# Column chunks of both array halves side by side in the expert weights of block 1

## The chip, the cores and the metric

The kernel runs on one core of a Trainium2 chip. The metric is the time of one execution on the device in microseconds (us); less is better. Before the change, three runs gave a median of 2655.25 us (2653.65 to 2655.34).

## The reference, cut to what matters

Two transformer blocks follow one another on 256 tokens of 1024 channels, in float32. The change touches the feed-forward part of block 1: 16 experts, each of which takes its best 34 tokens and applies a gated product with a hidden width of 2816.

```python
def _expert_choice_ffn(h, norm_g, w_router, w_gate, w_up, w_down):
    ...
    hid = (jax.nn.silu(jnp.einsum('becd,edf->becf', xs, w_gate))
    ...
```

So for every expert `silu(xs @ w_gate) * (xs @ w_up)` is formed, [tokens, 2816], and multiplied with `w_down` [2816, 1024]. Each hidden column goes through this on its own, and the sum over hidden columns may be taken in any order. Block 2 has a context stream (256 context tokens, whose only product is a few states of two recurrences) and a latent stream, which needs block 1's output.

## The kernel before, in words

The kernel has three parts. `head` is block 1's token mixer and router. `ffn` (L787) is block 1's experts, and in the same stage the context stream of block 2 (`ctx_pre`, from L885), which depends on no expert. `lat` is the rest of block 2 and waits for the last expert's result.

An expert (`expert`, L836) has room for 64 tokens, so a product fills only half of TensorE's columns. Two products therefore run on the two halves of the array. The 2816 hidden columns are cut in two halves of 1408; the lower half of the array takes the first, the upper half the second. A loop over three chunks takes 512, 512 and 384 columns of each half. For each chunk, `w_gate` and then `w_up` are multiplied with the tokens: eight k-tiles of 128 channels, at each the product of half 0 and then that of half 1 (`gu`, L848). Then come the sigmoid on ACT and two products on DVE (`hid`), transposes (`hb`, L858), a copy (`hT`), and the second product into `dn` (L866). The next expert's tokens are gathered (`xg`, `xt`, `ohb`) in the second chunk, and `sc` (L879, L880) adds the result to the tokens. A float32 matmul of the program stands in the trace as two.

Weights come through ten slots of 8 KB a partition (1 MB each), which are used in turn; the first expert has four more. `wload` (L223) loads [1024, n] weights. For n of 512 or 384 it puts four k-tiles of one half into one slot:

```python
        kk = SLOTW // n if n <= 256 else 4
        kk = min(kk, KD)
```

So a chunk of `w_gate` comes in four loads: half 0 with k-tiles 0 to 3, half 0 with 4 to 7, then the same of half 1. A row of such a load is 2048 B (512 columns) or 1536 B (384). `rload` (L244) loads rows of `w_down`, 4096 B each, two k-tiles a slot; the 384 rows of a half's third chunk take one full and one half-filled slot. Loads are issued on SP's queue, in the program's order, and a load waits there until the last matmul that read its slot is done.

The order of the instructions on each engine is fixed when the program is built: a scheduler puts them in order by its own estimate of when each could start, and so spreads the context stream's work between the experts' matmuls. On the chip every engine runs its list in order. The context stream's work on PE is, in this order: projections (`pc`), an inverse by steps (`gic`, `gib`, `giy`; later `r0ic`, `r0ib`, `r0iy`), and scans (`gp`; `rp`). Each step's matmul waits for DVE or ACT to have processed the step before. A step of the inverse on PE (L1104) is one of three: with `gY` (or `rY`) as the first operand, then with `giZ` (`r0iZ`), then with `ctab`.

Of the kernel before, what the change touches and what calls it, by code (L numbers as in the profile page):

```python
# [50 lines left out]
# blocks of 2048 modulation columns and channel tiles, in the order in which they are taken  # L51
# [4 lines left out]
# weight slots that the first expert has besides  # L56
RX = 4
# products queued behind those of the solves and scans: of the next column tile, and others
# [26 lines left out]
def const_table():  # L85
# [3 lines left out]
    # pairs of neighbouring blocks of 2^l  # L89
# [54 lines left out]
class Ring(list):  # L144
    """pools of weight slots, used in turn"""
# [7 lines left out]
class Net:  # L153
    def __init__(self, tc, I, out, ctx, ring=4):
# [7 lines left out]
        # what the mixers alone need, apart  # L162
# [19 lines left out]
    def add_ring(self, ctx, name, n):  # L182
        """n weight slots of 8 KB a partition, handed out in turn with those that are there"""
        pool = ctx.enter_context(self.tc.tile_pool(name=name, bufs=n, reuse_waits="tile"))
        self.rings = Ring(self.rings + [pool] * n)

    @contextmanager
    def phase(self, **banks):
        """PSUM banks by tag, for a part of the kernel"""
        old = self.rings, self.ptag  # L190
        with ExitStack() as ctx:
            self.pspool = {t: ctx.enter_context(self.tc.tile_pool(name=t, bufs=n, space=PSUM, reuse_waits="tile")) for t, n in banks.items()}
            yield ctx
        self.rings, self.ptag = old

    @contextmanager
    def side(self, pool, tag):
        """emit with weight slots of `pool` and the PSUM banks of `tag`"""
# [24 lines left out]
    def wload(self, src, n):  # L223
        """[1024, n] weights as a function of the k-tile and the columns"""
        kk = SLOTW // n if n <= 256 else 4
        kk = min(kk, KD)
# [7 lines left out]
    def loader(self, bufs):  # L234
        """128 columns of block 2's input projection (or n of src) at a time, into bufs of 4 KB a partition in turn"""
# [9 lines left out]
    def rload(self, src):  # L245
        """rows of 1024 columns, 128 a k-tile"""
# [9 lines left out]
    def split(self, src, hi, lo, eng=None):  # L256
        """an exact split of float32 values in two parts of fewer bits"""
        self.nc.scalar.copy(hi, src)  # L258
        (eng or self.nc.vector).tensor_sub(lo, src, hi)  # L259
        return hi, lo  # L260

    def product3(self, out, pairs):
        """out = the sum of a^T b over pairs of operands in two parts each; the product of the second parts is below
        the last bit"""
# [5 lines left out]
    def sigmoid(self, out, x, scale=1.0, nbias=None):  # L270
        """1 / (1 + exp(-(scale x + bias))); nbias holds -bias"""
# [5 lines left out]
    def rsqrt_cols(self, out, x, scale, bias):  # L277
        """out = (x*scale + bias) ** -0.5 through exp and ln."""
# [4 lines left out]
    def evac(self, out, src, scale=None, eng=None):  # L283
        """PSUM to SBUF, alternating between ACT and DVE."""
# [12 lines left out]
    def head(self):  # L297
        tc, nc, I = self.tc, self.nc, self.I
        ring = self.rings[0]
        # the weights' slots of both parts of the block  # L300
# [13 lines left out]
    def norm_rows(self, W, src, tag):  # L314
        """x * rsqrt(mean(x^2) + eps) for the token tiles in src."""
# [16 lines left out]
    def to_T2(self, W, src, gain, name):  # L332
        """token tiles -> [128, 8, 272] in two parts, channel on partitions, scaled per channel; the meta tokens also whole"""
# [13 lines left out]
    def wgroup(self, src, c):  # L347
        """256 columns of [1024, n] weights, whole and in two parts"""
# [9 lines left out]
    def metas(self, W, um, raw):  # L358
        """[16, 256]: the meta tokens' products with whole weights, the channels in four parts at once"""
# [10 lines left out]
    def head_body(self, W):  # L370
# [31 lines left out]
        # log_sigmoid of the decay logits, on every partition  # L402
# [4 lines left out]
        def rvt(t, name):  # L407
            """in place of states to come, where there are any"""
# [10 lines left out]
        # projections, channel-major  # L419
# [25 lines left out]
        # decayed scores of the retention  # L445
# [10 lines left out]
        # token-major projections  # L456
# [6 lines left out]
        def projN(c0, out):  # L463
            """256 columns of all tokens at a time"""
# [21 lines left out]
        # retention  # L486
# [34 lines left out]
        # what bars a direction from the tokens on its other side, in place of the distances  # L521
# [3 lines left out]
        # the gates' columns in two parts, spread so that the two directions start at partitions 0 and 32  # L525
# [6 lines left out]
        # gates  # L532
# [35 lines left out]
        # matrix memory: weighted scores of both directions, and the sums over them a head later  # L568
# [62 lines left out]
        # output projection and residual; the retention's gate on the way  # L631
# [28 lines left out]
        # the router's logits on the way: products with the channels as they come, the norm's factor later  # L660
# [31 lines left out]
    def head_norm(self, W, out, src, n, name):  # L692
        """(x - mean) * rsqrt(var + eps) over each of four heads of 128."""
# [11 lines left out]
    def log_sigmoid(self, W, out, x, n, m, name):  # L705
        """min(x, 0) - log1p(exp(-|x|))"""
# [11 lines left out]
    def route(self, W, h, lT):  # L718
        """softmax over experts, the best CAP tokens of each, one-hot maps."""
# [58 lines left out]
    def norm_factor(self, W, x, junk, t, n):  # L778
        """rsqrt(mean(x^2) + eps) of the rows of a token tile"""
# [9 lines left out]
    def ffn(self):  # L789
        with self.front, self.phase(pa=6, pb=2) as ctx:  # L790
# [4 lines left out]
            # more slots at first, in place of the context's tiles to come  # L795
# [9 lines left out]
    def gather(self, W, e):  # L805
        """the tokens of an expert, channel-major, and the way back"""
        nc = self.nc
        # one-hot rows of the places, twice: for both halves of the channels
# [27 lines left out]
    def expert(self, W, e, tokens):  # L836
# [4 lines left out]
        for c, (f0, w) in enumerate(((0, 512), (512, 512), (1024, 384))):  # L841
            gu = []
            for src in (I["w_gate"], I["w_up"]):
                b = self.bank("gu")
                ws = [self.wload(src[0, e, :, h * (DFF // 2) + f0:h * (DFF // 2) + f0 + w], w) for h in range(2)]
                for k in range(KD):
                    for h in range(2):
                        nc.tensor.matmul(b[h * 64:(h + 1) * 64, :w], xs[:, k, :], ws[h](k),  # L848
# [11 lines left out]
            self.evac(hT[:, :nf], hb[:, :nf], eng="v" if c % 2 else "s")  # L860
            for h in range(2):
                r0 = h * (DFF // 2) + f0
                wd = self.rload(I["w_down"][0, e, r0:r0 + w, :])
                for j in range(nf):
                    for dc in range(2):
                        nc.tensor.matmul(dn[dc * 64:(dc + 1) * 64], hT[:, j, h * 64:(h + 1) * 64],  # L866
                                         wd(j, slice(dc * 512, (dc + 1) * 512)),
# [18 lines left out]
    def ctx_pre(self):  # L886
        """modulation vectors and the states that the context stream leaves behind"""
# [7 lines left out]
        with tc.tile_pool(name="CW", bufs=2, reuse_waits="tile") as CW, self.side(CW, "pb"):  # L895
            with tc.tile_pool(name="C", bufs=1, reuse_waits="tile") as C:
                with tc.tile_pool(name="C0", bufs=1, reuse_waits="tile") as T:
                    # what the shift adds to the logits of the routing to come
# [27 lines left out]
    def ada(self, W):  # L926
        """modulation vectors of both streams: channel columns, and the rows that gate the residuals; a step per weight slot"""
# [19 lines left out]
        def close(c):  # L947
            """rows of 512 columns at every 32nd partition, for the context one partition on"""
# [41 lines left out]
    def gate_rows(self, which, out):  # L990
        """broadcast one residual gate over the partitions: [128, 1024]"""
# [10 lines left out]
    def mod_cols(self, W, gain, r, shift, scale, name):  # L1002
        """gain * (1 + scale) and shift as channel columns."""
# [7 lines left out]
    def norm256(self, W, src, dst, name):  # L1011
        """dst = src * rsqrt(mean(src^2) + eps) for two token tiles [128, 1024]"""
# [11 lines left out]
    def affT(self, W, src, gs, sh, name, tag=None, ptags=None):  # L1024
        """two token tiles -> [128, 8, 256] with channels on partitions, times gs plus sh"""
# [15 lines left out]
    def projc(self, w, uT):  # L1041
        """[128 channels, 256 tokens] of one column tile; a step per product"""
# [6 lines left out]
    def advance(self, queue, n):  # L1049
        """emit n steps of what waits in a queue"""  # L1050
# [9 lines left out]
    def fill(self, ins, *steps):  # L1060
        """products that wait for nothing, behind an instruction whose result takes its time"""
# [4 lines left out]
    def softplus(self, W, x, n, m, name):  # L1066
        """x <- max(x, 0) + log1p(exp(-|x|))"""
# [11 lines left out]
    def mixed_inverse(self, W, N, U, d, Y, levels, pfx, hop=lambda ins: None):  # L1079
        """Y = (I + N)^-1 of four strictly triangular 128-blocks [128, 4, 128], in blocks of up to 2^levels. A step per  # L1080
        product.
# [1116 lines left out]
```

## Time and profile before, and how to read it

| what | value |
|---|---|
| median of three runs | 2655.25 us |
| the profiled execution: span from first to last instruction | 2657.6 us |
| the experts' stage (first `gu` to last `sc`), from the span's start | 320.7 to 1854 us |
| PE busy, of the span | 2371.7 us (89%) |
| DVE, ACT, POOL busy | 1145.6, 651.1, 473.6 us |
| loaded by SP's queue | 747.67 MB |
| `gu` matmuls (L848) | 3072, 731.4 us |
| `dn` matmuls (L866) | 1408, 321.1 us |

The profile is one execution, and it gives the span alone as that execution's time. PE is TensorE's matmuls, PEld its weight loads. An engine's busy time is the time in which at least one of its instructions runs. "DMA share" is the mean busy share of the core's 16 DMA engines; as transfers overlap on an engine, it can be over 1. The granted clock is given as a share of full speed (1.00 is 2.4 GHz, and the lower level is 1.2 GHz).

### The profile page before, as it was taken

The page shows a single profiled execution, that of the slowest core. Times are in us where ns is not written, and L with a number is a line of the kernel's source. Part 1 is how long each engine was busy: PE and PEld are TensorE (multiplying, and loading weights), DVE is VectorE, ACT ScalarE, POOL GpSimd, SP SyncE. Part 2 cuts the span into 40 slices and gives each one's busy share as a digit, 9 for nine tenths or more (in the row PEclk, how much of TensorE's full clock was granted, in tenths as well). Part 3 has the DMA queues.
Part 4 walks back from the last instruction along what each step waited for, and adds up shares of the span by engine and source line. Part 5 has one row for each costly group of instructions (what it writes and reads, how often), then busy time and mean ns, then how long its engine had stood idle before and what let it go on. Part 6 is the DMA issues. An engine that isn't in the chain of part 4 may idle for free. (4 is left out here: it accounts for less than half of the span.)

```text
span 2657.6 us, 37500 instructions
## 1 busy us (share of the span) xinstructions
PE 2371.7 (89%) x14784; PEld 1268.7 (48%) x14784; DVE 1145.6 (43%) x2515; ACT 651.1 (24%) x1652; POOL 473.6 (18%) x657
## 2 busy tenths in 40 slices
PE   6879799999999998989989988887898988989997
PEld 5746434334334334334333332222766676876554
DVE  7786311332332333233323321011677866565555
ACT  3334111210211212112112211001453443522222
POOL 5671100100001111011101100000434442210000
PEclk9878899999999999999999999999899999999999
DMA  6537899998989999999989999999221111589995
GB/s 205 188 129 240 287 387 387 385 369 309 382 320 359 354 339 359 358 329 374 359 319 356 368 332 390 394 391 356 70 74 42 28 49 41 169 285 349 365 365 196
DMA packets 426708, 754.58 MB, mean 284 GB/s; under 512 B 13344, under 2 KB 233168, under 8 KB 423456
## 3 DMA queue, kind: packets, MB, share of 16 engines
q1 hardware_dynamic: 425024, 747.67, 79.2%
q0 software_dynamic: 1504, 4.46, 0.5%
q8 instruction: 119, 1.95, 0.3%
q14 instruction: 61, 0.50, 0.1%
HBM read 751.03 MB, written 1.05 MB: 283 GB/s over the span
## 5 line engine op out<-in xcount | busy, mean ns | idle before, releaser
L848 PE MATMUL gu<-w,xs 128*64 128x512 f32 (+1 forms) x3072 | 731.4, 584 | 33.5 <-DMA w<-in_w_up 19.9
L848 PEld LDWEIGHTS gu<-w,xs 128*64 128x64 f32 x3072 | 232.6, 142 | 418.9 <-issue 362.1
L866 PE MATMUL dn<-w,hT 128*64 128x512 f32 x1408 | 321.1, 597 | 11.6 <-ACT hT L290 10.4
L866 PEld LDWEIGHTS dn<-w,hT 128*64 128x64 f32 x1408 | 95.3, 136 | 183.5 <-issue 160.3
L1045 PE MATMUL pc<-luT,w 128*128 128x256 f32 x688 | 176.5, 399 | 1.4 <-DMA w<-in_w_in 1.1
L1045 PEld LDWEIGHTS pc<-luT,w 128*128 128x128 f32 x688 | 127.6, 195 | 23.9 <-issue 4.5
L273 ACT ACTIVATE hid<-gu 128x512 f32<-128x512 f32 (+1 forms) x48 | 26.9, 561 | 403.2 <-PE gu L848 403.2
L2054 PE MATMUL egu<-w,exs 128*64 128x256 f32 x1024 | 123.2, 383 | 0.0
L853 DVE TENSOR_TENSOR hid<-hid,gu 128x512 f32<-128x512 f32 (+1 forms) x48 | 30.7, 639 | 208.9 <-ACT hid L275 208.8
L854 DVE TENSOR_TENSOR hid<-hid,gu 128x512 f32<-128x512 f32 (+1 forms) x48 | 30.8, 643 | 195.3 <-PE gu L848 195.2
L1589 POOL TENSOR_SCALAR rsw<-rSU,rwc 64x64 f32<-64x64 f32 x112 | 40.5, 362 | 332.5 <-DVE rSU L1603 323.5
L2054 PEld LDWEIGHTS egu<-w,exs 128*64 128x64 f32 x1024 | 74.6, 136 | 39.4 <-issue 6.9
L268 PE MATMUL pj<-uTh,wp 128*128 128x272 f32 x320 | 68.3, 308 | 12.1 <-DVE rtmp L441 7.5
L1045 PE MATMUL pc<-cuT,w 128*128 128x256 f32 x288 | 70.3, 392 | 0.0
L2081 PE MATMUL edn<-w,ehT 128*64 128x512 f32 x256 | 67.7, 597 | 0.7 <-ACT ehT L290 0.5
L258 ACT CAST wp<-w 128x1024 fp32r<-128x1024 f32 (+1 forms) x48 | 55.4, 1186 | 49.3 <-DMA w<-in_w_in 33.8
L1098 DVE TENSOR_TENSOR r0iZ<-r0ic,stab 128x512 f32<-128x512 f32 x48 | 32.9, 686 | 78.7 <-PE r0ic L1104 78.6
L259 DVE TENSOR_TENSOR wp<-w,wp 128x1024 fp32r<-128x1024 f32 (+1 forms) x44 | 62.6, 1447 | 9.8 <-ACT wp L258 9.8
L1547 PE MATMUL rmt<-rT,rBK 128*128 128x128 f32 (+1 forms) x256 | 49.8, 341 | 18.7 <-DVE rBK L1515 5.6
L981 POOL TENSOR_TENSOR adac<-adac,w 128x2048 f32<-128x2048 f32 x14 | 66.1, 4722 | 0.3
L1045 PEld LDWEIGHTS pc<-cuT,w 128*128 128x128 f32 x288 | 53.5, 193 | 19.1 <-issue 10.6
L268 PEld LDWEIGHTS pj<-uTh,wp 128*128 128x128 f32 x320 | 55.2, 205 | 14.4 <-issue 8.1
(686 smaller groups left out, 3740.5 us busy)
## 6 DMA issues: line engine op xcount, KB each, us to landing
w<-in_w_down SPq DMA_DIRECT2D x160, 1024.0 KB, 11.4
w<-in_w_gate SPq DMA_DIRECT2D x128, 1024.0 KB, 10.3
w<-in_w_up SPq DMA_DIRECT2D x128, 1024.0 KB, 11.6
w<-in_w_gate SPq DMA_DIRECT2D x64, 768.0 KB, 8.3
w<-in_w_up SPq DMA_DIRECT2D x64, 768.0 KB, 7.1
w<-in_w_in SPq DMA_DIRECT2D x65, 512.0 KB, 4.1
w<-in_moe_w_gate SPq DMA_DIRECT2D x32, 1024.0 KB, 13.4
w<-in_moe_w_up SPq DMA_DIRECT2D x32, 1024.0 KB, 12.1
```

The lines of the kernel that those rows point to most:

```text
L258: self.nc.scalar.copy(hi, src)
L259: (eng or self.nc.vector).tensor_sub(lo, src, hi)
L268: self.nc.tensor.matmul(out, a[x], b[y], start=(i == 0 and x + y == 0), stop=(i == n - 1 and x == 1))
L848: nc.tensor.matmul(b[h * 64:(h + 1) * 64, :w], xs[:, k, :], ws[h](k), start=(k == 0), stop=(k == KD - 1))
L866: nc.tensor.matmul(dn[dc * 64:(dc + 1) * 64], hT[:, j, h * 64:(h + 1) * 64], wd(j, slice(dc * 512, (dc + 1) * 512)), start=(c == 0 and h = ...
L981: nc.gpsimd.tensor_add(acc[c], acc[c], w)
L1045: self.nc.tensor.matmul(b, w(k), uT[:, k, :], start=(k == 0), stop=(k == KD - 1))
L1098: nc.vector.tensor_tensor(out.rearrange("p u (i c) -> p u i c", i=4), x.unsqueeze(2).to_broadcast([P, 4, 4, 32]), blk, op=ALU.mult)
L1547: ins = nc.tensor.matmul(b[:, i], BK[:, c0 + i, h:h + 2, :], T[:, h, c0 + i, :, :], start=True, stop=True)
L1589: nc.gpsimd.tensor_scalar(sw[r], SU[r, h, c, :], wc[r, c:c + 1], 0.0, op0=ALU.mult, op1=ALU.add)
L2054: nc.tensor.matmul(b[64 * i:64 * i + 64, x * 256:x * 256 + 256], xs[:, k, i, :], w[i](k), start=(k == 0), stop=(k == KD - 1))
L2081: nc.tensor.matmul(b[64 * i:64 * i + 64, :], hT[:, j, 64 * i:64 * i + 64], wd[i](j, cs), start=(j == 0), stop=(j == 1))
```

## The change

The two halves of the array take neighbouring columns. The chunks are now of 1024, 1024 and 768 neighbouring hidden columns; in each chunk half 0 takes the first 512 (or 384) columns and half 1 the next. `wload` is called once for both halves, and loads two k-tiles of 1024 (768) columns into a slot, in rows of 4096 (3072) B. The rows of `w_down` are taken in the same new order, 1024, 1024 and 768 at a time. Every product is still formed, over other groups of columns.

```diff
     def wload(self, src, n):
-        kk = SLOTW // n if n <= 256 else 4
-        kk = min(kk, KD)
+        kk = min(SLOTW // n, KD)
...
-        for c, (f0, w) in enumerate(((0, 512), (512, 512), (1024, 384))):
+        for c, (f0, w) in enumerate(((0, 512), (1024, 512), (2048, 384))):
...
-                ws = [self.wload(src[0, e, :, h * (DFF // 2) + f0:h * (DFF // 2) + f0 + w], w) for h in range(2)]
+                ws = self.wload(src[0, e, :, f0:f0 + 2 * w], 2 * w)
                 for k in range(KD):
                     for h in range(2):
-                        nc.tensor.matmul(b[h * 64:(h + 1) * 64, :w], xs[:, k, :], ws[h](k),
+                        nc.tensor.matmul(b[h * 64:(h + 1) * 64, :w], xs[:, k, :], ws(k, slice(h * w, (h + 1) * w)),
...
+            wd = self.rload(I["w_down"][0, e, f0:f0 + 2 * w, :])
             for h in range(2):
-                r0 = h * (DFF // 2) + f0
-                wd = self.rload(I["w_down"][0, e, r0:r0 + w, :])
                 for j in range(nf):
...
-                                         wd(j, slice(dc * 512, (dc + 1) * 512)),
+                                         wd(h * nf + j, slice(dc * 512, (dc + 1) * 512)),
```

The other users of `wload` have 256 columns, for which the number of k-tiles in a slot stays eight.

The scheduler orders the changed program differently. Three places show it.

The first is PE in the third expert, in the context stream's first inverse (`gic`). Before:

```order
L866 MATMUL dn<-w,hT 64x512 x16
L1104 MATMUL gic<-ctab,giB 32x128 x4
L848 MATMUL gu<-w,xs 64x512
L1104 MATMUL gic<-gY,giB 32x128 x4
L1104 MATMUL gic<-giZ,giB 32x128 x4
L1104 MATMUL gic<-ctab,giB 32x128 x4
L1104 MATMUL gic<-gY,giB 32x128 x4
L1104 MATMUL gic<-giZ,giB 32x128 x4
L1104 MATMUL gic<-ctab,giB 32x128 x4
L1104 MATMUL gic<-gY,giB 32x128 x4
L848 MATMUL gu<-w,xs 64x512 x8
```

The same in the changed program:

```order
L1103 MATMUL gic<-gY,giB 32x128 x4
L848 MATMUL gu<-w,xs 64x512 x4
L1103 MATMUL gic<-giZ,giB 32x128 x4
L1103 MATMUL gic<-ctab,giB 32x128 x4
L848 MATMUL gu<-w,xs 64x512 x4
L1103 MATMUL gic<-gY,giB 32x128 x4
L848 MATMUL gu<-w,xs 64x512 x4
L1103 MATMUL gic<-giZ,giB 32x128 x4
L1103 MATMUL gic<-ctab,giB 32x128 x4
L848 MATMUL gu<-w,xs 64x512 x4
```

Before, a `gu` group begins with one matmul alone (that of half 0 at the first k-tile), and the rest follows in pieces of seven, eight or more. Now the pieces are of four, the matmuls that read one slot. Counted from the first expert's `gu` to the context stream's last matmul on PE:

| on PE, in the program's order | before | changed |
|---|---|---|
| pieces of `gu` between other work | 184 | 208 |
| of these, pieces of a single matmul | 50 | 1 |
| L1104 step with `giZ`/`r0iZ` with no expert's matmul ahead of it since the step it depends on (of 48) | 14 | 1 |
| the step with `gY`/`rY`, likewise (of 48) | 16 | 12 |
| the step with `ctab`, likewise (of 36) | 11 | 15 |
| `hb` straight behind `gu` | 4 | 7 |
| `dn` straight behind `hb` | 7 | 11 |

The second place is PE at the end of the context stream's work, the last scan steps (`rp`). Before, this stands in the 13th expert's third chunk:

```order
L1599 MATMUL rp_10638<-rSU_10470,rKt_10477 64x64 x2
L1579 MATMUL rp_10647<-rSU_10470,rT_8614 64x64 x2
L1593 MATMUL rp_10655<-rP_10650,rY_10494 64x64 x2
L848 MATMUL gu<-w,xs 64x384 x8
L1599 MATMUL rp_10655<-rSU_10470,rKt_10477 64x64 x2
L848 MATMUL gu<-w,xs 64x384 x7
L858 MATMUL hb<-ctab,hid 128x128 x3
L866 MATMUL dn<-w,hT 64x512 x12
L879 MATMUL sc<-yhi,ohT 128x512 x4
```

In the changed program it stands in the 12th expert's first chunk:

```order
L848 MATMUL gu<-w,xs 64x512 x4
L1578 MATMUL rp_10615<-rSU_10438,rT_8582 64x64 x2
L1592 MATMUL rp_10623<-rP_10618,rY_10462 64x64 x2
L858 MATMUL hb<-ctab,hid 128x128 x4
L1598 MATMUL rp_10623<-rSU_10438,rKt_10445 64x64 x2
L865 MATMUL dn<-w,hT 64x512 x16
L848 MATMUL gu<-w,xs 64x512 x32
L858 MATMUL hb<-ctab,hid 128x128 x4
```

From there to the end of the stage PE has experts' work alone: before for the rest of one chunk and three experts, now for two chunks and a `dn` and four experts.

The third place is SP's queue at the end of the stage. Before, the third chunk of the last expert's `w_down` comes in four loads, two of them half-filled, and two loads of block 2's `w_in` stand ahead of the last:

```order
L252 DMA w<-in_w_down 128x2x1024
L252 DMA w<-in_w_down 128x1024
L252 DMA w<-in_w_down 128x2x1024
L241 DMA w<-in_w_in 128x8x128 x2
L252 DMA w<-in_w_down 128x1024
L241 DMA w<-in_w_in 128x8x128 x4
```

In the changed program these are three full loads, and `w_in` comes behind them:

```order
L251 DMA w<-in_w_down 128x2x1024 x4
L229 DMA w<-in_w_gate 128x2x768 x4
L229 DMA w<-in_w_up 128x2x768 x4
L251 DMA w<-in_w_down 128x2x1024 x3
L240 DMA w<-in_w_in 128x8x128 x6
```

Behind the stage the order of the work is as it was, but for a few rows.

## Rows read from the trace of the kernel before

**Rows 1.** The page's head.

```profile
span 2657.6 us, 37500 instructions
```

**Rows 2.** Windows of the experts' stage: us, busy us of each engine, PEclk, DMA share, GB/s.

```profile
318.00:583.00 265.00, 251.59 (x1283) 104.53 (x1284) 66.84 (x151) 47.78 (x109) 12.27 (x14) 0.97 1.04 379
583.00:1583.50 1000.50, 915.13 (x5359) 383.39 (x5361) 320.56 (x707) 179.47 (x447) 122.04 (x253) 0.97 0.96 348
1583.50:1854.00 270.50, 221.89 (x986) 73.92 (x982) 28.04 (x47) 23.84 (x40) 0.58 (x1) 0.96 1.04 387
```

**Rows 3.** Waits of PE, 318 to 1583.5 us: total us, times, longest us.

```profile
PE r0ic L1104 <- DVE r0iZ L1098: 8.2, 10, 0.9
...
PE hb L858 <- DVE hid L854: 7.2, 16, 0.8
...
PE dn L866 <- ACT hT L290: 6.0, 12, 1.0
...
PE gic L1104 <- DVE giZ L1098: 4.9, 7, 0.9
...
PE r0ic L1104 <- DVE r0iB L1128: 2.9, 7, 0.4
...
PE gic L1104 <- ACT giB L1123: 1.9, 4, 0.5
```

**Rows 4.** Waits of PE, 1583.5 to 1854 us, the two longest.

```profile
PE gu L848 <- DMA w<-in_w_up: 19.9, 8, 3.8
PE gu L848 <- DMA w<-in_w_gate: 13.2, 9, 3.5
```

**Rows 5.** Windows in which one row length was loaded: 2048, 1536, 4096 and 512 B.

```profile
1612.50:1632.00 19.50, 14.98 (x66) 4.64 (x66) 0.69 (x1) 1.95 (x3) 0.00 (x0) 1.00 1.05 387
1645.00:1659.00 14.00, 12.93 (x66) 4.75 (x62) 1.09 (x3) 0.27 (x1) 0.00 (x0) 1.00 1.06 373
1602.50:1610.50 8.00, 7.83 (x36) 2.37 (x32) 0.82 (x2) 1.95 (x3) 0.00 (x0) 1.00 1.03 410
...
320.00:323.00 3.00, 2.70 (x16) 1.04 (x16) 1.66 (x6) 0.00 (x0) 0.00 (x0) 1.00 1.21 294
```

**Rows 6.** Timeline of PE, 586 to 600 us: start us, us, instruction.

```profile
586.99 3.65 PE L848 MATMUL gu<-w,xs 128*64 128x512 f32 x16
590.57 0.42 PE L1104 MATMUL gic<-ctab,giB 128*32 128x128 f32 x8
590.92 3.65 PE L848 MATMUL gu<-w,xs 128*64 128x512 f32 x14
594.50 0.43 PE L1104 MATMUL gic<-gY,giB 128*32 128x128 f32 x8
594.86 1.07 PE L848 MATMUL gu<-w,xs 128*64 128x512 f32 x2
595.86 0.43 PE L1104 MATMUL gic<-giZ,giB 128*32 128x128 f32 x8
```

**Rows 7.** Timeline of PE, first expert, without context work.

```profile
320.70 14.01 PE L848 MATMUL gu<-w,xs 128*64 128x512 f32 x64 [0.30 <-DVE xs L827]
...
336.82 7.09 PE L866 MATMUL dn<-w,hT 128*64 128x512 f32 x32 [0.69 <-ACT hT L290]
343.74 13.90 PE L848 MATMUL gu<-w,xs 128*64 128x512 f32 x64
...
369.59 10.54 PE L848 MATMUL gu<-w,xs 128*64 128x384 f32 x64
...
389.44 2.18 PE L903 MATMUL ebs<-crw,mcol 128*128 128x36 f32 x16
```

**Rows 8.** Timeline of PE where the context stream's work ends.

```profile
1583.37 0.28 PE L1599 MATMUL rp<-rSU,rKt 128*64 128x64 f32 x4
1583.48 2.75 PE L848 MATMUL gu<-w,xs 128*64 128x384 f32 x14
```

**Rows 9.** Timeline of SP near the stage's end.

```profile
1833.96 8.43 SPq L241 DMA_DIRECT2D w<-in_w_in  x2
```

## The prediction

> **What bounds the kernel now.** The profiled execution has a span of 2657.6 us [rows 1], 2.4 us above the median of the three runs, 2655.25. The sum is made against the span, and its difference is taken from the median.
>
> The change touches only the experts' stage, 318 to 1854 us, so I looked there first with windows by stage [rows 2], then at what PE waited for in them. The reader is to see two regimes. Up to 1583.5 us, while the context stream's work lies between the experts' matmuls, PE is busy for 1166.7 of 1265.5 us, and the waits that PE has are for ACT and DVE, in short pieces of a microsecond or less [rows 3]; no wait for a weight is among them. From 583 on the DMA share is 0.96, against 1.04 to 1.06 where the engines are saturated [rows 2, 5]: transfers have slack, PE sets the pace. From 1583.5 on the experts are alone: the DMA share is 1.04, and PE waits 33.1 us for `w_gate` and `w_up` [rows 4]. There the transfers set the pace. I call these the mixed stretch (1265.5 us) and the tail (270.5 us).
>
> So faster transfers can only pay in the tail, and what the change does to PE's list decides the mixed stretch. The two are tied: the changed order ends the context's work earlier, in the 12th expert instead of the 13th, so 1.7 experts move from the stretch where PE is the bound to the one where transfers are.
>
> **1. Transfer rate by row length.** Windows with one row length show 373 GB/s at 1536 B, 387 at 2048, 410 at 4096 [rows 5]. Over 16 engines that is 65.9, 84.7 and 159.8 ns a row. A straight line through the last two (9.5 ns a row, and 75.1 ns for each 2048 B) gives 65.8 ns for 1536 B, as measured, so I trust it for 3072 B: 122.3 ns, 402 GB/s, an estimate from these rows. An expert is 16.78 MB of `gate` and `up` in chunks of 512, 6.29 MB in the chunk of 384, and 11.53 MB of `down`. Before: 43.4 + 16.9 + 28.1 = 88.4 us. Changed: 40.9 + 15.7 + 28.1 = 84.7 us, 3.7 us less.
>
> The page "DMA: Bandwidth & Descriptors" of the Trainium skill (Specifications) puts the least transfer for line rate at 512 B and over, by which longer rows would gain nothing here. The three windows disagree with it; what it would make of the time is the second rival.
>
> **2. The tail.** Where the context's work ends before [rows 8], 14 of the trace's 64 `up` matmuls of the 13th expert's last chunk are left, so about 1.57 MB of `up`, 3.15 MB of `down` and three experts are still to be consumed: 4.2 + 7.7 + 3 x 88.4 = 277.1 us of transfer (the stretch took 270.5; the difference is what had landed ahead). Changed, there are left the 12th expert's second and third chunk of `gate` and `up` (8.39 MB at 410, 6.29 at 402: 20.5 + 15.7), all of its `down` (28.1) and four experts: 64.3 + 4 x 84.7 = 403.1 us. With as much landed ahead, the tail grows by 126.0. The two `w_in` loads no longer stand ahead of the last `down`: 2 x 0.524 MB at 294 GB/s [rows 5, 9] is 3.6 us less. Net +122.4. PE's own work for an expert, 68.7 us from 320.70 to 389.44 [rows 7], stays under 84.7, so the tail stays bound by transfers.
>
> **3. The mixed stretch.** (a) Moved matmuls. The first expert, without context work, prices them: its chunks took 23.0, 25.9 and 19.9 us, the first chunk's `dn` 6.9 [rows 7]. Moved out are the 12th expert's first `dn` and two chunks (52.7) and the 13th's two chunks and 50 of 64 of the last `gu` (23.0 + 25.9 + 8.2 = 57.1): -109.8 us.
>
> (b) Lone matmuls. Before, `gu` often begins with a single matmul, two in the trace. It takes 1.00 us until the next work starts (594.86 to 595.86); and the piece of 14 that completes a group takes 3.58, as much as a whole piece of 16 [rows 6]. So a lone matmul costs its full 1.00 us, with one half of the array idle. In chunks of 384, which are a third, I take three quarters of that. 50 such pieces become 1: 49 x 0.92 = -45 us. The ends are 0 (if other work had waited in any case) and 49.
>
> (c) More pieces. Without the lone ones `gu` is in 134 pieces before and 207 now. A piece of 16 takes 3.58 us [rows 6], in an unbroken run 16/64 of 13.90, 3.47 [rows 7], so a change of work costs 0.11 us, and 73 more cost 8 us. The ends are 0 and the 0.57 us that a lone matmul pays above its share (1.00 less 2 x 0.217), 42 us. I take 8, since whole k-tiles fill both halves as the pieces of 16 do.
>
> The page "TensorEngine Tiling (Array Packing)" of the Trainium skill (Key Properties) says that a change of tiling mode drains the engine, which speaks against finer pieces. The pieces of 16 show the drain at 0.11 us, the lone ones at 0.57; by the latter for every piece the whole sum would end 34 us higher.
>
> (d) Context steps with nothing to cover them. For the `giZ` step the wait was 13.1 us in 17 times, 0.77 each [rows 3]; steps with no expert's matmul ahead go from 14 to 1: -10. The `gY` step: 4 fewer by 0.48; the `ctab` step: 4 more by 0.41; `hb` straight behind `gu`: 3 more by 0.45; `dn` straight behind `hb`: 4 more by 0.50 [rows 3]: together +3. Net -7. The ends are -20 (the scans' waits shrink too) and +10 (new ones appear).
>
> (e) At nothing: the shorter rows' saving in the mixed stretch (PE waits for no weight there), the sixteen `down` loads that fall away on SP's queue (hidden by the same slack), and slots that are freed after 4 matmuls instead of after half a group, which lets loads start earlier; if transfers were bound there, these would count. The granted clock, 0.97 on average [rows 2], I leave as it is: about 6% of the stretch at 1.2 GHz.
>
> Sum for the stretch: -109.8 - 45 + 8 - 7 = -153.8, so 1111.7 us, 98 us an expert, still above the 84.7 of transfers and the few context loads.
>
> **Sum.** -153.8 + 122.4 = -31.4 us: the stage ends at 1822.6 instead of 1854, the span is 2626.2. What follows it keeps its order, and I cost it at nothing. From the median: 2655.25 - 31.4 = 2623.9, so **2624 us**.
>
> **The rivals.** *Slower: the context's chain, not PE's load, sets the mixed stretch.* Then the lone matmuls and the covered steps give nothing, since PE would have waited for DVE and ACT anyway, while the tail still grows: -109.8 + 8 + 122.4 = +20.6, 2676 us. It decides as soon as (b) and (d) give less than the 20.6 that they must make up. For it: nearly 100 us of PE's waits in the stretch are for such steps, and they would be packed closer in time. Against: PE is busy 92% of the stretch, and 1.00 us for two matmuls is seen with more work ready behind them.
>
> *The row length buys nothing*; the tail then runs at the old rates: the 12th expert's rest is 21.7 + 16.9 + 28.1 = 66.7, with four experts at 88.4 420.3 us, 17.2 more than in 2. The sum is -14, 2641 us. For it: the line is drawn through windows of 8 to 20 us. Against: they repeat at each expert.
>
> *Transfers bind everywhere*: the mixed stretch shrinks until its transfers have no slack, because the granted clock rises as PE's gaps close (half-speed stretches cost about 3%, some 38 us). Every expert then gains its 3.7 us: 16 x 3.7 = 59, 2596 us. Against: nothing in the rows says which gap lowers the clock.
>
> *No change*: half of (b) and none of (d) come, 2655 less a few us. It would need the 50 lone pieces to be mostly where PE had nothing else ready.
>
> **How the numbers follow.** A measurement of this kernel tells differences of about 0.2%, 5 us, from none. Forecast (-31, its own band from -50 to -8 by the ends in 3): 0.60. Slower: 0.12. Rows buy nothing: 0.06. Transfers bind everywhere: 0.14. No change: 0.08. So faster 0.80, same 0.08, slower 0.12. The range reaches from the case of transfers everywhere, with 3 us to spare, to the edge of no change: 2593 to 2656; outside lie the slower case and a little of the fastest, under 2 in 10.
>
> **What would show it.** Windows with `gate` rows of 4096 B near 410 GB/s, and of 3072 B near 402. The context's last `rp` on PE near 1430 us, with PE busy over 90% before it and no wait for a weight there. A tail of about 393 us at a DMA share near 1.03, with PE's wait for weights longer than 33 us. Pieces of eight `gu` matmuls that take about 1.8 us to the next work. `giZ` waits of 1 or 2 us in all instead of 13. The prediction is wrong if the last `rp` stands later than about 1460 us (then (b) or (d) failed), or if PE waits for weights in the mixed stretch (then the transfers had no slack), or if the tail is shorter or longer than 393 by more than 10 us.

## The result and the profile after

The changed kernel takes 2591.89 us (median of 4 runs, 2591.54 to 2596.49) against 2655.30 us of the kernel before in the same comparison: a ratio of 0.9763, with a 95% interval of 0.9750 to 0.9776. It is faster by 63.4 us. The forecast was faster by 31.4 us, so the sign was right and the size half; 2592 lies 1 us under the range's lower end of 2593. The profiled execution has a span of 2590.2 us, 67.4 less than [rows 1].

The page of the changed kernel, its head and the group of the `gu` matmuls:

```profile
span 2590.2 us, 37494 instructions
...
L848 PE MATMUL gu<-w,xs 128*64 128x512 f32 (+1 forms) x3072 | 678.0, 571 | 42.8 <-DMA w<-in_w_up 27.9
```

Windows of the experts' stage, with the boundary where the context's work now ends; the columns are those of [rows 2]:

```profile
318.00:583.00 265.00, 251.07 (x1389) 103.52 (x1388) 76.41 (x163) 50.87 (x116) 14.38 (x18) 0.99 1.01 390
583.00:1390.90 807.90, 748.84 (x4694) 318.88 (x4690) 295.79 (x661) 164.23 (x418) 120.09 (x249) 0.99 0.93 354
1390.90:1785.00 394.10, 325.21 (x1493) 100.03 (x1495) 41.47 (x75) 35.99 (x61) 0.58 (x1) 1.00 1.03 405
```

The mixed stretch ends at 1390.9 instead of 1583.5 us. The tail has grown from 270.5 to 394.1 us and is bound by transfers as before: its DMA share is 1.03, and it now moves 405 GB/s instead of 387. In the middle window the DMA share fell from 0.96 to 0.93, so the transfers did not become the bound there. One column moved that the prediction had left alone, PEclk, the mean granted clock: 0.97 became 0.99.

The same boundaries on PE's timeline, first `gu` and last `rp`, and between them two pieces of eight, each the work of one slot:

```profile
309.75 15.07 PE L848 MATMUL gu<-w,xs 128*64 128x512 f32 x62
...
507.86 1.94 PE L848 MATMUL gu<-w,xs 128*64 128x512 f32 x8
509.73 0.43 PE L1103 MATMUL gic<-giZ,giB 128*32 128x128 f32 x8
...
1376.68 1.94 PE L848 MATMUL gu<-w,xs 128*64 128x512 f32 x8
1378.44 0.29 PE L1598 MATMUL rp<-rSU,rKt 128*64 128x64 f32 x4
...
1390.55 0.34 PE L1598 MATMUL rp<-rSU,rKt 128*64 128x64 f32 x4
```

Against [rows 7, 8] the first `gu` starts 11 us earlier. A piece of eight takes 1.76 us until an `rp` of the same shape (`128*64`) starts, and 1.87 us until a `gic` (`128*32`) does. Its share of an unbroken run is 1.74 us (8/64 of 13.90 [rows 7]). So finer pieces that fill both halves cost up to 0.13 us a piece, near the 0.11 that the prediction took from pieces of 16.

PE's waits from 310 to 1390.9 us, the lines that answer to [rows 3]:

```profile
PE dn L865 <- ACT hT L289: 10.4, 19, 1.1
PE hb L858 <- DVE hid L854: 10.3, 16, 2.8
...
PE r0ic L1103 <- DVE r0iB L1127: 3.7, 9, 0.4
...
PE gic L1103 <- DVE giZ L1097: 1.0, 1, 1.0
...
PE r0ic L1103 <- DVE r0iZ L1097: 0.9, 1, 0.9
```

The `giZ` waits of [rows 3], 13.1 us in 17 times, are 1.9 us in two; `hb` and `dn` wait 7.5 us longer in all. And the waits for weights in the tail, which answer to [rows 4]:

```profile
PE gu L848 <- DMA w<-in_w_up: 27.9, 48, 1.2
PE gu L848 <- DMA w<-in_w_gate: 14.5, 25, 0.6
```

They are 42.4 us instead of 33.1, in many short pieces instead of a few long ones; a slot now holds work for 1.8 us.

Stage by stage, with each end read from PE's timeline:

| us | before | after | difference | forecast |
|---|---|---|---|---|
| until the first `gu` | 320.7 | 309.75 | -11 | 0 |
| mixed stretch | 1262.9 | 1081.1 | -181.8 | -153.8 |
| tail | 271.0 | 395.3 | +124.3 | +122.4 |
| behind the stage | 802.9 | 804.0 | +1 | 0 |

So two things were to be explained: 28 us in the mixed stretch, and 11 us that are there before anything changed runs (the first expert's first weight load is issued at 267.53 us before and at 256.14 after). And the prices that came out near had to be shown to be right for their reasons. My theory (A in the expectations) was the prediction's own: PE's list sets the mixed stretch, and the row length counts only where transfers are the bound. An expert that stands in the tail costs 84.7 us with long rows and 88.4 with short ones, in the stretch 68.7.

### The profile page after: what moved, and what is told of

Read it like the earlier page. It is cut to its first block, busy times and chain, and to the rows that moved or that the text cites. A ratio compares the mean times of both kernels' runs of the same rounds, so it can differ in the third digit from the quotient of the medians.

```text
span 2590.2 us, 37494 instructions
## 1 busy us (share of the span) xinstructions
PE 2314.5 (89%) x14784; PEld 1233.4 (48%) x14784; DVE 1144.0 (44%) x2515; ACT 651.8 (25%) x1652; POOL 474.0 (18%) x657
## 3 DMA queue, kind: packets, MB, share of 16 engines
HBM read 751.03 MB, written 1.05 MB: 290 GB/s over the span
## 5 line engine op out<-in xcount | busy, mean ns | idle before, releaser
L848 PE MATMUL gu<-w,xs 128*64 128x512 f32 (+1 forms) x3072 | 678.0, 571 | 42.8 <-DMA w<-in_w_up 27.9
L848 PEld LDWEIGHTS gu<-w,xs 128*64 128x64 f32 x3072 | 202.3, 138 | 384.9 <-issue 264.8
L865 PE MATMUL dn<-w,hT 128*64 128x512 f32 x1408 | 329.0, 604 | 22.8 <-ACT hT L289 15.8
L272 ACT ACTIVATE hid<-gu 128x512 f32<-128x512 f32 (+1 forms) x48 | 26.9, 560 | 359.1 <-PE gu L848 359.1
L854 DVE TENSOR_TENSOR hid<-hid,gu 128x512 f32<-128x512 f32 (+1 forms) x48 | 30.9, 643 | 146.8 <-PE gu L848 145.4
## 6 DMA issues: line engine op xcount, KB each, us to landing
w<-in_w_up SPq DMA_DIRECT2D x128, 1024.0 KB, 13.1
```

## The experiments

### Short rows in the changed kernel's slots

Both halves still share a slot, but two transfers fill it, one k-tile each, in rows of 2048 and 1536 B. The edit, against the changed kernel's `wload`, cut to the loads:

```
-    t = self.wslot()[:, :kk * n].rearrange("p (k c) -> p k c", k=kk)
-    self.dma.dma_start(t, src[...])
+    t = self.wslot()[:, :4 * w].rearrange("p (h k c) -> p h k c", h=2, k=2)
+    for k in range(2):
+        self.dma.dma_start(t[:, :, k], src[(k0 + k) * P:(k0 + k + 1) * P, :].rearrange("p (h c) -> p h c", h=2))
```

> The slots of the changed kernel (two k-tiles of both halves in one), but each slot is filled by two transfers of one k-tile each, whose rows are 2048 and 1536 B as before the change. On TensorE there is no lone matmul left, 259 pieces of gu instead of 200 until the context's last inverse, and that inverse stands 0.83 of an expert earlier (10.25 instead of 11.08). Theory A (TensorE's own order sets the mixed stretch, the row length counts in the tail alone): first gu at 310 us, stretch 1081 - 0.83 x 68.7 + 59 x 0.11 = 1031 us, tail 5.5 experts x 88.4 = 486 us, 804 us behind it: a span of 2631, a time of about 2633 us. Theory B (the longer rows bring the whole gain): back to about 2655 us. Theory C (the order brings all, the row length nothing): the tail at 84.7 us an expert, 466 us, a time of about 2612 us.

Measured: 2628.0 us, ratio 0.9902 (0.9884 to 0.9921). The two windows, mixed stretch and tail:

```profile
311.90:1329.00 1017.10, 956.99 (x5820) 398.43 (x5822) 360.45 (x810) 208.83 (x521) 134.49 (x267) 0.98 0.99 357
1329.00:1817.10 488.10, 408.12 (x1792) 109.87 (x1788) 51.77 (x94) 43.79 (x74) 0.84 (x2) 1.00 1.04 388
```

The tail of 488 us is theory A's 486, at 388 GB/s as before the change, though each transfer is half as large: the row length sets the rate. The stretch is 1017 us, 14 less than A gave: short rows cost nothing there. Nearly all of the 14 us is idle time of PE, 60.1 us against the changed kernel's 73.1. B's 2655 and C's 2612 both fall. The rows bring their gain, but only in the tail; the order brings its own without them.

### Neighbouring columns alone

The halves take neighbouring columns, but each is loaded by itself, four k-tiles at a time, as before.

```
-    ws = self.wload(src[0, e, :, f0:f0 + 2 * w], 2 * w)
+    ws = [self.wload4(src[0, e, :, f0 + h * w:f0 + (h + 1) * w], w) for h in range(2)]
```

> Neighbouring columns for the two halves, but each half's weights still in slots of their own with four k-tiles in rows of 2048 and 1536 B, all loads of the lower half first, as before the change. 42 lone matmuls and 169 pieces of gu until the context's last inverse (before: 48 and 178), which stands 0.33 of an expert earlier (12.33 instead of 12.67). Theory A: stretch -0.33 x 68.7 - 6 x 0.92 - 9 x 0.11 = -29 us, tail +0.33 x 88.4 = +29 us: about 2655 us, within 8. Rival (which columns lie side by side is itself worth something, without longer rows and without whole slots): below 2640 us.

Measured: 2654.45 us against 2655.11, ratio 0.9993 (0.9977 to 1.0008), no difference. The stretch was 1232.7 us (-30.2; A gave -29) and the tail 298.1 (+27.1; A gave +29). Which columns lie side by side is worth nothing by itself. The run also shows the exchange plainly: the context ended a third of an expert earlier, and the stretch gave to the tail what it saved.

### Loads of the two halves in turn

As in the run before, but the two halves' loads alternate. The edit is against that run, cut to the loop:

```
     for k0 in range(0, KD, 4):
+        for h in range(2):
-        self.dma.dma_start(t, src[k0 * P:(k0 + 4) * P, :].rearrange("(k p) c -> p k c", p=P))
+            self.dma.dma_start(t, srcs[h][k0 * P:(k0 + 4) * P, :].rearrange("(k p) c -> p k c", p=P))
```

> As the run with the old loads, but the loads of the two halves alternate: lower four k-tiles, upper four, lower, upper. The context's last inverse stands at 10.12 experts, as in the run with short rows (10.25); rows are as long as there and pieces of gu nearly as many (272 against 259), but 90 of them are lone matmuls, where that run has none. So the pair prices a lone matmul. Theory A (0.92 us each, on the path): stretch 1031 + 90 x 0.92 + 13 x 0.11 - 0.13 x 68.7 = 1106 us, tail 497 us, time about 2719 us, 86 us above the run with short rows. Rival (a lone matmul costs nothing there, since it stands in time in which TensorE would wait): about 2636 us, within 10 of that run.

Measured: 2676.2 us, ratio 1.0081 (1.0062 to 1.0099), slower than before the change. The counts in this expectation are not those of the kernel that ran, which has 72 lone matmuls and 187 pieces of `gu` until the last inverse, at 10.93 experts. So the comparison with the run of short rows does not hold as it was written. The run stands beside the changed kernel instead (1 lone, 200 pieces, last `rp` at 11.33 experts; here 11.10). Windows of stretch and tail, and PE's timeline of some lone matmuls:

```profile
314.30:1437.00 1122.70, 1047.73 (x6063) 440.69 (x6065) 370.57 (x826) 213.42 (x530) 133.52 (x267) 1.00 0.96 344
1437.00:1863.00 426.00, 343.15 (x1553) 117.42 (x1551) 43.39 (x78) 38.53 (x65) 0.72 (x2) 1.00 1.04 389
```

```profile
584.85 3.65 PE L857 MATMUL gu<-w,xs 128*64 128x512 f32 x14
588.43 0.43 PE L1112 MATMUL gic<-giZ,giB 128*32 128x128 f32 x8
588.78 1.07 PE L857 MATMUL gu<-w,xs 128*64 128x512 f32 x2
589.78 0.43 PE L1112 MATMUL gic<-ctab,giB 128*32 128x128 f32 x8
```

The signature is that of [rows 6]: 1.00 us for the lone one, 3.58 for the piece of 14. By A's prices from the changed kernel, 0.23 of an expert less is -15.8, 13 fewer pieces -1.4, and 71 lone matmuls at 0.92 are +65.3: a stretch of 1129 us, measured 1122.9. Solved for the lone matmul, (1122.9 - 1081.1 + 15.8 + 1.4) / 71 is 0.83 us; with the difference in time at half clock (3.4 us here, 23.9 there, at most half of it lost) it is up to 0.98 us. The tail by A is 395.3 + 0.23 x 88.4 + 4.67 x 3.7 = 433 us, measured 425.9. The rival, that a lone matmul is free, falls: the 71 cost about 59 us.

### Before and after, profiled once more

> The kernel before, unchanged, profiled a second time, for what varies from one execution to the next. If the head (the time until the first gu) and the stretches at a granted clock of 0.50 are chance, the first gu falls anywhere from 310 to 321 us and the half-clock time of the mixed stretch (64.9 us) and of the head (92.2 us) comes out otherwise; if they belong to the kernel, they come again: 319 to 321 us, 65 us in 12 to 14 pieces.

> The changed kernel, unchanged, profiled a second time. If the shorter head and the 23.9 us of half clock in its mixed stretch belong to the kernel, the first gu comes at 309 to 312 us again with some 24 us in 7 pieces; if they are chance, they may come out as before the change: 320 us and 65 us.

Measured: 2654.3 and 2601.2 us, one run each. First `gu` and the windows of stretch and tail, of the kernel before:

```profile
312.20 2.37 PE L848 MATMUL gu<-w,xs 128*64 128x512 f32 x10 [0.30 <-DVE xs L827]
```

```profile
312.20:1581.20 1269.00, 1170.04 (x6630) 489.62 (x6632) 386.94 (x856) 226.68 (x554) 134.40 (x267) 0.97 0.97 353
1581.20:1852.30 271.10, 223.02 (x982) 74.36 (x978) 28.25 (x48) 24.05 (x41) 0.80 (x2) 0.95 1.05 387
```

and of the changed kernel:

```profile
314.14 2.37 PE L848 MATMUL gu<-w,xs 128*64 128x512 f32 x10 [0.30 <-DVE xs L826]
```

```profile
314.10:1393.80 1079.70, 1006.62 (x6111) 424.55 (x6111) 373.41 (x828) 215.31 (x534) 134.73 (x267) 0.99 0.95 364
1393.80:1788.40 394.60, 324.88 (x1499) 99.47 (x1499) 42.08 (x76) 36.23 (x62) 0.81 (x2) 1.00 1.03 405
```

The head (the time until the first `gu`) is chance: this time it is 312.2 us before and 314.1 after, the other way round. It goes with the clock only roughly: the heads of 320.7, 309.75, 312.2 and 314.1 us hold 92, 75, 72 and 72 us at a granted clock of 0.50. So the 11 us belong to neither kernel. The work behind the stage varies as well: 802.9 and 800.2 us before, 804.0 and 811.0 after, with PE idle for 73 to 74 us in all four and 81, 78, 92 and 105 us at half clock. In the changed kernel's second profile the two are 11 us longer than in its first, which is why its time, 2601.2 us, lies 9 us above the median.

The stretch is not chance. It is 1269.0 and 1079.7 us, within 6 of the first profiles. Its time at half clock comes out much as it did: 75.1 us before (64.9 the first time), 23.9 us after (23.9, without the last 3 us of a piece that began in the head). The falls come at the same places of the program: after the change at 422.0, 500.5, 722.4, 831.6, 1033.0, 1183.2 and 1330.0 us, in the second profile each of them 2.8 or 2.9 us later. Before the change, all 13 falls of the first profile come again in the second, and three are added.

### The context's steps held back

The table of stages shows what the change left lying: the tail pays 84.7 us an expert for transfers, in which PE works 68.7. The context's twelve scan steps were put on PE's queue behind products of later experts; no instruction is added. The edit is against the changed kernel, cut to one of its two kinds of step:

```
+    with self.hold(4 + 2 * j + d):
         self.rwkv_back(j, d, x, self.rwkv_front(j, d, x, env), env)
...
+    with self.tc.issue_after(self.marks[round(3 * (HOLD[0] + HOLD[1] * i)) - 1].ins):
+        yield
```

`marks` holds the last `dn` of every chunk of every expert; HOLD is 2.3, 1.05.

> The changed kernel, with each of the context's twelve scan steps held back on TensorE's queue behind a product of a later expert, so that the last inverse stands at 14.33 experts instead of 11.08 (211 pieces of gu until there, 2 of them lone). No instruction is added or taken away. Theory A (the stretch is set by TensorE's own work, the tail by transfers, in which TensorE idles about 16 us an expert): 3.25 experts move out of a tail that pays 84.7 us each into a stretch that pays 68.7: -52 us, about 2540 us (2530 to 2565), DMA share of the stretch up from 0.93 to about 0.95. Rival (TensorE and the transfers are each already a bound in the stretch, so spreading the context only moves the waits): within 10 of 2592 us; and if the held steps stand uncovered, above it.

Measured: 2531.2 us, ratio 0.9542 (0.9519 to 0.9565), the fastest of all. The windows of stretch and tail:

```profile
312.80:1600.70 1287.90, 1213.87 (x7144) 497.76 (x7146) 406.97 (x880) 243.24 (x576) 134.32 (x267) 0.99 1.01 391
1600.70:1721.20 120.50, 98.93 (x468) 31.26 (x464) 13.11 (x24) 10.70 (x19) 0.83 (x2) 1.00 1.03 399
```

By the last `rp`, 3.26 experts moved (11.33 to 14.59). The stretch grew by 206.8 us, 63 an expert, the tail shrank by 274.8, 84 an expert. The DMA share of the stretch went further than A had it, to 1.01, still without a wait for `gate` or `up` in it.

### The hold with short rows

The edit is that of the short rows, on the run with the hold.

> The run with the held context steps, with rows of 2048 and 1536 B (two transfers to a slot, as in the run with short rows); the context's last inverse stands at 14.33 experts as there, with 286 pieces of gu until it instead of 211. In that run the DMA share of the stretch was already 1.01, with 391 GB/s, and 1.03 with 399 to 404 GB/s where TensorE waits for weights. Theory A (row length costs wherever transfers are near their limit, so now in the stretch too): the stage of the experts moves 552 MB, 1422 us at the 388 GB/s of short rows, so its 1408 us become at least 1422 and, with the ends not covered, up to 1440: a time of 2545 to 2565 us, and PE waits for weights in the stretch of more than 30 us. Rival (row length counts only after the context's end): 75 x 0.11 + 1.41 x 3.7 = 13 us, with no more waits for weights than the 12 us of that run: about 2544 us.

Measured: 2554.2 us, ratio 0.9615 (0.9599 to 0.9631). The windows of stretch and tail:

```profile
317.90:1616.00 1298.10, 1223.81 (x7128) 483.49 (x7130) 402.50 (x879) 240.22 (x574) 133.69 (x267) 0.99 1.04 385
1616.00:1753.00 137.00, 111.05 (x486) 28.62 (x481) 13.74 (x25) 12.60 (x22) 0.78 (x2) 1.00 1.04 382
```

The profiled execution is the slowest of the four (2562.8 us). Its stage takes 1435 us, within A's 1422 to 1440, and the stretch is now saturated at 1.04 and 385 GB/s. By the medians 23 us are lost against long rows, where the rival gave 13. But the sign that A named did not come: waits for weights in the stretch are 11.4 us, not 30, and PE's idle time there is 74 us in both runs. The 10 us by which the stretch is longer are busy time, with 30.7 us at half clock against 17.1 and 75 more pieces; the other 16 us stand in the tail (137.0 against 120.5). So short rows cost more under the hold than the rival's prices give, but that they cost in the stretch itself is not shown.

### The hold spread further, and less

HOLD is 2.3, 1.12, and then 2.3, 0.97.

> The run with the held context steps, with the steps spread further, so that the context's last inverse stands at 15.04 experts instead of 14.33. Theory A (each expert that moves from the tail into the stretch gains 84.7 - 68.7 = 16 us): 0.71 x 16 = -11 us, about 2520 us. Rival (transfers are at their limit all along by now, share 1.01, so what moves changes nothing): 2531, within 5.

Measured: 2542.5 us (2538.0 to 2546.9), 11 us slower than the first hold where 11 faster was expected. The tail went to 58.9 us, but the stretch grew by 70.9 for 0.74 of an expert, 96 us an expert. Neither theory named that; the rival, that transfers leave nothing to gain, is the nearer. By A's price 0.74 of an expert is 51 us; of the 20 us above it 17 are idle time of PE (91.1 us against 74.0), with `hb` waiting 26.9 us for `hid` instead of 14.9.

> The run with the held context steps, spread less, so that the last inverse stands at 13.33 experts instead of 14.33. With 15.04 experts the time was 2542.5 us, 11 us above the 2531 us at 14.33. If the best place lies between, where the DMA share of the stretch first reaches that of the tail (1.03): each expert given back to the tail costs 84.7 - 68.7 = 16 us: about 2547 us (2540 to 2552). Rival (the share of 1.01 at 14.33 experts is already the limit, so that the best place lies earlier): 2531 us or below.

Measured: 2588.6 us, against both theories; three of the four executions took 2588 to 2589 us, one 2571.4. The windows of stretch and tail:

```profile
319.00:1574.90 1255.90, 1164.73 (x6827) 476.16 (x6829) 396.51 (x865) 234.38 (x563) 134.79 (x267) 0.98 0.98 374
1574.90:1779.50 204.60, 168.19 (x787) 52.04 (x783) 22.16 (x39) 18.49 (x32) 0.81 (x2) 1.00 1.03 401
```

The tail is as priced (84.1 us more for one expert). But the stretch is only 32 us shorter than at 14.33 experts, where A gives 68.7: 37 us too long. PE's idle time in it is 91 us against 74, with waits of up to 3.6 us for `hid`, and 47.8 us stand at half clock against 17.1, of which at most half, 15 us, is lost. So the place where the context ends does not fix the time alone; the waits that a spread leaves, and the clock, do as well. Why this spread leaves more of them was not tried.

### The hold on the kernel before

> The kernel before, without any part of the change, with its context steps held back in the same way, so that the last inverse stands at 14.34 experts instead of 12.67, with 55 lone matmuls and 184 pieces instead of 48 and 178. If the hold is worth the same without the change (an expert in the stretch 68.7 us, in the tail 88.4): stretch 1.67 x 68.7 + 7 x 0.92 + 6 x 0.11 = +122 us, tail -1.67 x 88.4 = -148 us: -26 us, about 2629 us (2620 to 2640). Rival (what the hold brings depends on the whole slots and long rows of the change): within 5 of 2655 us.

Measured: 2615.2 us against 2660.6 in that comparison, ratio 0.9832 (0.9809 to 0.9856), -45 us: the forecast's direction, with more than its size (2629 us, 2620 to 2640). The tail shrank by 156 us (A gave 148), the stretch grew by 114 (A gave 122, from the mean of the two profiles, 1266). So the hold pays without the change too, and the change pays with it: 2531 against 2615.

## Why the prediction was half right

**1, the rate by row length: right.** In the tail of the changed kernel, windows with one row length, 4096 and 3072 B:

```profile
1533.50:1574.00 40.50, 30.94 (x132) 8.20 (x130) 2.06 (x3) 4.49 (x7) 0.00 (x0) 1.00 1.02 409
1586.00:1598.00 12.00, 11.35 (x64) 4.47 (x62) 1.45 (x4) 1.63 (x3) 0.00 (x0) 1.00 1.03 399
```

409 and 399 GB/s, forecast 410 and 402. The page "DMA: Bandwidth & Descriptors" of the Trainium skill (Specifications), by which rows of 512 B and over are all at line rate, differs from this and from [rows 5]; the measurement decides.

**2, the tail: right**, +124.3 and, in the second profiles, +123.5 us for +122.4. That transfers set it is shown by the run with short rows, whose tail came out at its own price. One reading in it is loose: of the 64 matmuls of that last chunk only 32 are of `up`; half of that `up`, the 1.57 MB taken, fits 14 of 32 to half a microsecond.

**3a to 3c, PE's list: right in kind.** PE's busy time in the stretch is the fairest test, since it leaves the waits out. Before and after:

```profile
320.70:1583.50 1262.80, 1165.00 (x6630) 487.28 (x6632) 386.91 (x856) 226.67 (x554) 134.31 (x267) 0.97 0.97 355
```

```profile
309.70:1390.90 1081.20, 1008.15 (x6111) 425.19 (x6111) 373.44 (x828) 215.10 (x534) 134.47 (x267) 0.99 0.95 363
```

It fell by 156.9 us; (a), (b) and (c) gave -109.8 - 45 + 8 = -146.8. The lone matmul's price of 0.92 us is borne out by the run that made 71 more of them (0.83 to 0.98). The change of work is priced rightly too: at full clock, all 21 pieces of eight with 512 columns in the changed kernel's stretch that work of the same shape (`128*64`) follows at once take 1.72 to 1.77 us, their share of an unbroken run, and those before any other shape take 1.82 to 1.87, up to 0.13 more. The page "TensorEngine Tiling (Array Packing)" of the Trainium skill (Key Properties) has the engine drained when the tiling mode changes, not just the tile; the trace agrees, at 0.13 us or less. The 0.57 us of a lone matmul, which the prediction read as a drain, is another thing: a pair of both halves takes 0.87 us in an unbroken run (13.90 for 16 pairs [rows 7]), and the lone one takes 1.00, so only 0.13 us of it go with the change of work, and the rest is the idle half.

**3d, the uncovered context steps: right in kind, mis-sized.** This is the step that failed most. Idle time of PE in the stretch, from the same two rows, fell from 97.8 to 73.1 us: -24.7 us where I took -7, and beyond the end of -20 that I had kept. In the second profiles it fell by 25.9. The `giZ` part came as counted (-11.2), and `hb` and `dn` wait 7.5 us longer, where I had 3. What I had not sized made up the rest: by PE's waits in the stretch, the inverse's other steps fell from 31.9 to 21.7 us, the scans (`gp`, `rp`), which I had kept in the bound alone, from 22.6 to 14.7, and the other waits by 3.4. The waits of `rp`, before and after:

```profile
PE rp L1599 <- ACT rSU L1596: 7.2, 9, 1.4
...
PE rp L1579 <- DVE rSU L1603: 7.0, 11, 2.5
PE rp L1593 <- ACT rP L1582: 6.3, 12, 1.4
```

```profile
PE rp L1598 <- ACT rSU L1595: 5.5, 9, 0.7
...
PE rp L1592 <- ACT rP L1581: 4.5, 11, 0.7
PE rp L1578 <- DVE rSU L1602: 4.4, 10, 0.5
```

**3e, the granted clock "I leave as it is": wrong.** This is the other step that failed: the term was put at nothing. Time at half clock (0.50, that is 1.2 GHz) in the stretch fell from 64.9 to 23.9 us, in the second profiles from 75.1 to 23.9. PE was busy for 57.8 and 67.9 us of it before and for 23.6 us after, and at half clock at most half of busy time is lost, so at most 17 and 22 us came from there. One fall in the kernel before, PE's timeline and the windows around it:

```profile
1130.81 1.02 PE L848 MATMUL gu<-w,xs 128*64 128x512 f32 x2
1137.40 3.75 PE L1547 MATMUL rmt<-rT,rBK 128*128 128x128 f32 x16 [5.58 <-DVE rBK L1515]
```

```profile
1131.00:1135.00 4.00, 0.83 (x2) 0.00 (x0) 3.18 (x9) 1.41 (x4) 3.27 (x7) 1.00 1.05 376
1135.00:1142.00 7.00, 4.60 (x19) 3.79 (x21) 4.04 (x10) 0.96 (x3) 1.99 (x5) 0.51 1.04 400
1142.00:1146.00 4.00, 4.00 (x22) 1.40 (x20) 2.46 (x6) 0.67 (x2) 1.79 (x2) 1.00 0.51 148
```

PE ran out of work behind a lone matmul and waited 5.58 us for DVE; the clock fell in that wait, and the work after it ran at 1.2 GHz until 1142 us. Here the wait is paid twice. It is not so for every fall: that at 422.0 us in the changed kernel follows on 32 matmuls of 16 columns, with PE never idle in the 12 us before it.

```profile
417.91 3.75 PE L1164 MATMUL gab<-wab,cuT 128*128 128x16 f32 x32
421.59 5.35 PE L848 MATMUL gu<-w,xs 128*64 128x512 f32 x16
```

Together, 18 us more in idle time (3d) and 10 us more in busy time are the 28 us of the stretch that were missing; in the second profiles they are 19 and 17. The clock is enough for the busy part. No run holds the clock fixed, so its exact share stays open: by its bound, (b) or (c) may be too favourable by up to 7 us.

The head's 11 us are chance. Head and work behind the stage differ by -11 and +1 us in the first pair of profiles and by +2 and +11 in the second. Only the stretch misses in both, by 28 and 36 us, against 32 between forecast and medians.

**The rivals.** "Transfers bind everywhere" gave 2596 us, the nearest number, for the wrong reason: the clock did rise, which the prediction had here and not in its sum, but transfers did not bind in the stretch (0.93; and short rows cost nothing there). "Rows buy nothing" falls by the tail's 405 GB/s, "the context's chain" and "no change" by the stretch: steps that found cover did shorten it.

## What to carry to other kernels

Where a stage has two regimes, price an instruction by the regime in which it stands: what leaves the PE-bound part for a transfer-bound tail is paid again there, at 84.7 us for 68.7 in this kernel, and spreading the covering work to the end (2531 us) was worth as much as the change itself. When a change closes waits of a TensorE stream, sum all of the stream's waits, not the largest group alone, and give the time at half clock a term with bounds instead of nothing. Profile both kernels a second time before a difference in untouched code is explained; here 11 us in the head were chance.

## What was not expected of the hardware

- Most falls of the clock belong to places of the program: the seven of the changed kernel's stretch came again in the second profile, at the same distances, and the 13 of the kernel before came again with three more. In the head and behind the stage the time at half clock varies (72 to 92 us and 78 to 105 us in four profiles).
- Between `gu` and other work, only a change of shape costs: 0.13 us or less after a piece of eight, nothing that shows where the next matmul has the same `128*64`.
- Lone matmuls do not by themselves lower the clock. The run with the halves' loads in turn has 72 of them and 3.4 us at half clock in its whole stretch (mean 1.00); the kernel before has 48 and 64.9 us. It also has 11.4 us of waits for `giZ` (13.1 in the kernel before) and 5.6 us of waits for `rBK` (5.6, there in one piece, here in three), so neither sum explains the falls. What decides whether a wait ends in one stays open.
- Half as many bytes in a row at a saturated queue cost 6 to 7% (409 against 387 GB/s for 4096 and 2048 B, 399 against 373 for 3072 and 1536), and nothing that shows in the changed kernel's mixed stretch, where the share was 0.95 with long rows.
